# The first matmuls of a down projection set between the last two products of an FFN part

## The chip, the cores and the metric

The kernel runs on one core of a Trainium2 chip. The metric is the device time of one execution in microseconds (us), the median of several runs. Engines are called by their short names: PE is the matmul engine (PEld its weight loads), ACT the scalar engine, DVE the vector engine, POOL the GpSimd engine, SP the engine whose queue issues the DMAs here.

## What is computed

The program is one inference step of a two-layer decoder. Each layer is a mixer, an FFN and a gated addition, for 576 token columns (512 of a prompt, 64 of samples) and a model width of 1024. The change lies in the FFN:

```python
def _swiglu(x, w1, w3, w2):
    return (jax.nn.silu(x @ w1) * (x @ w3)) @ w2

x = x + _swiglu(_rmsnorm(x, W['g_ffn'][i]), W['ffn_w1'][i], W['ffn_w3'][i], W['ffn_w2'][i])
# D_MODEL = 1024, D_FF = 2816, DEPTH = 2
```

The residual `x` is held as eight tiles of 128 rows (features) by 576 columns (tokens). All of it is float32.

## The kernel before, in words

**Precision.** Every float32 operand of a matmul is split into a high part (a rounded copy made by ACT) and a low part (the rest, made by DVE), and each product is three matmuls: high by high, low by high, high by low. `split_to` (L159, L160) does so for activations, `wsplit` (L174, L175) for weights: one ACT copy of 128x1024 into `whi`, one DVE subtraction into `wlo`. There are two buffers of each of `whi` and `wlo`, two of `wraw` (the weights as they land), two accumulators of two PSUM banks (`mm`, `mmx`) and one buffer each of the sums `a0` to `a3` and `u`.

**The up half.** The 22 tiles of the hidden width are worked in 11 pairs p. For each pair seven block products are made instead of eight (a Strassen scheme over the halves of tokens and of the inner width): the products with the operands b11, b21, b2, b1, b3, b4 and b22, each 24 matmuls of 288 columns (`prod`, L1120). Those with b11, b2, b3 and b4 add into the same accumulator (`mmx`); b21 goes to `mmy`, b1 and b22 to `mmz`. The weights of b2, b1, b3 and b22 are sums of loaded blocks, made by DVE (L1157, L1158, L1163, L1173) from a11, a12, a21, a22 (buffers a0, a1, a2, a3). Before b4 may add into `mmx`, ACT has to copy out what stands there (`copied`, L1125), since the copy is a result of its own. Between b3 and b4 the program puts the first product of the next pair (`head(p + 1)`), which works in the other accumulator.

**The down half.** The pairs are grouped in three parts (`PARTS`: 4, 4 and 3 pairs). After the last pair of a part the product with w2 follows: for each of eight output tiles m, `gemm` (matmuls at L210) loads and splits the block of w2, makes 48 matmuls (36 in the third part) over the part's eight (six) hidden tiles k, and `add_out` (L361) adds the two halves of the accumulator to x on DVE. The last operand k comes from the last product, b22, through a chain on DVE and ACT (L1135, L1136, L1138, L159, L160). The last pair of a part has no next head to put between b3 and b4.

**Order.** A list scheduler with a model of the engines sets the order on every engine queue, from the program's order and its own estimate of when each instruction can start; each engine then runs its queue in that order, and SP its DMAs. The two loops run in the two layers, so there are six parts, each with its last pair and its down half.

Of the kernel before, what the change touches and what calls it, by code (L numbers as in the profile page):

```python
# [12 lines left out]
F = mybir.dt.float32  # L13
R = mybir.dt.float32r
# [5 lines left out]
P = 128  # L20
D = 1024
KD = D // P
# [4 lines left out]
HF = T // 2  # L27
# [53 lines left out]
def trunk(ctx, tc, a, stop=None):  # L81
    nc = tc.nc
    V, S, G, PE = nc.vector, nc.scalar, nc.gpsimd, nc.tensor
# [82 lines left out]
    def wraw(ap, kt):  # L166
        raw = wp.tile([P, 1024], F, tag="raw", name="wraw", bufs=RAW)[:, :kt * P]
        nc.sync.dma_start(raw, ap)
        return raw
# [13 lines left out]
    def wload(ap, kt, eng=V):  # L183
        return wsplit(wraw(ap, kt), kt, wp, 2, eng=eng)
# [73 lines left out]
    def half(s):  # L258
        return slice(s * HF, (s + 1) * HF)
# [80 lines left out]
    def run(gen):  # L340
        for _ in gen:
            pass
# [10 lines left out]
    def add_out(m, ps, r=None):  # L353
        for s in range(2):
            xh, src = x[m][:, half(s)], ps[:, s]
            if r is not None:
                t = tmp("t1", 2)[:, :HF]
                V.tensor_tensor(t, src, r[:, half(s)], op=OP.mult)
                (V if m in OUT_V else G).tensor_tensor(xh, xh, t, op=OP.add)  # L359
            else:  # L360
                V.tensor_tensor(xh, src, xh, op=OP.add)  # L361
# [697 lines left out]
    def ffn(i, ha):  # L1059
        w13, w2 = a["w13"][i], a["w2"][i]  # L1060
        with tc.tile_pool(name=f"ffn{i}", bufs=1) as hp:

            def hq():
                return [hp.tile([P, 4, T], R, tag="h" + t_, name="h" + t_, bufs=2) for t_ in "hl"]

            def keep(n):
                if n < 3 or (n < 5 and i):
                    t = [ha.tile([P, 4, HF], R, tag=("bq" if n < 3 else "xb") + t_, name="b" + t_, bufs=WPRE if n < 3 else 2)
                         for t_ in "hl"]
                    return [(range(4), *t)]  # L1070
                if n < 5:
                    return [(range(2 * j, 2 * j + 2), *(ac.tile([P, 2, HF], R, tag="xc" + t_, name="b" + t_, bufs=KD // 2)
                                                        for t_ in "hl")) for j in range(2)]
                return [(range(j, j + 1), *(ac.tile([P, HF], R, tag="xa" + t_, name="b" + t_, bufs=KD)[:, None, :]
                                            for t_ in "hl")) for j in range(4)]

            def operand(n, src, scale=None):
                out = []
                for ks, hi, lo in keep(n):
                    split_to((hi, lo), src[:, ks[0]:ks[-1] + 1], scale)  # L1080
                    out += [(hi[:, j], lo[:, j]) for j in range(len(ks))]
                return out

            r = tmp("rb", 2)
            acc = tmp("acc", 1)
            for k in range(KD):
                square_add(acc, x[k], k == 0)
            rnorm([acc], D, 0, T, [(r, 1.0)])
            (xg0, t0), (xg1, t1) = ([t_.bitcast(F) for t_ in hq()] for _ in range(2))
            for xg, k0 in ((xg0, 0), (xg1, 4)):  # L1090
                for j in range(4):
                    V.scalar_tensor_tensor(xg[:, j], x[k0 + j], pcol("g_ffn", i * KD + k0 + j), r, op0=OP.mult, op1=OP.mult)  # L1092
                if k0 == 0:
                    b11 = operand(0, xg0[:, :, :HF])
            b21 = operand(1, xg1[:, :, :HF])
            d3, d2, d1, d4 = t0[:, :, :HF], t0[:, :, HF:], t1[:, :, :HF], t1[:, :, HF:]
            V.tensor_tensor(d3, xg1[:, :, HF:], xg0[:, :, HF:], op=OP.subtract)
            V.tensor_tensor(d2, d3, xg0[:, :, :HF], op=OP.add)
            b2 = operand(2, d2, -1.0)
            V.tensor_tensor(d1, xg0[:, :, :HF], xg0[:, :, HF:], op=OP.subtract)  # L1100
            b1 = operand(3, d1)
            b3 = operand(4, d3)
            V.tensor_tensor(d4, d2, xg1[:, :, :HF], op=OP.subtract)
            b4 = operand(5, d4)
            b22 = operand(6, xg1[:, :, HF:])

            def wsum(tag, src=None):
                t = hp.tile([P, 1024], F, tag=tag, name=tag, bufs=1)
                if src is not None:
                    nc.sync.dma_start(t, src)  # L1110
                return t

            def prod(outs, wts, b, first):
                wh, wl = wts
                for n in range(2):
                    for k in range(4):
                        o = slice(n * SEQ + k * P, n * SEQ + (k + 1) * P)
                        h, l = b[k]
                        for t_, (w, v) in enumerate(((wh, h), (wh, l), (wl, h))):
                            PE.matmul(outs[n], w[:, o], v, start=(first and k == 0 and t_ == 0), stop=(k == 3 and t_ == 2),  # L1120
                                      skip_group_check=not first)

            def copied(ps, tag):
                t = v2(tmp(tag, 2))
                S.activation(t, ps[:, :, :HF], AF.Copy)  # L1125
                return t

            def head(p):
                ps = pm.tile([P, 2, 512], F, tag="mm", name="mmx")
                prod([ps[:, n, :HF] for n in range(2)], wload(w13[p, 0], KD), b11, True)  # L1130
                return ps, copied(ps, "t1")

            def block(s, outs, dst, sign):
                for n in range(2):
                    V.tensor_tensor(s[:, n], s[:, n], outs[n], op=OP.add)  # L1135
                S.activation(s[:, 0], s[:, 0], AF.Silu, scale=sign)  # L1136
                if sign > 0:
                    V.tensor_tensor(dst, s[:, 0], s[:, 1], op=OP.mult)  # L1138
                else:
                    V.scalar_tensor_tensor(dst, s[:, 1], sign, s[:, 0], op0=OP.mult, op1=OP.mult)  # L1140

            for p0, p1 in PARTS:
                hs = []
                for p in range(p0, p1):
                    if p == p0:
                        ps, s1 = head(p)
                    if (p - p0) % 2 == 0:
                        hh, hl = hq()
                    o = 2 * ((p - p0) % 2)
                    xo = [ps[:, n, :HF] for n in range(2)]  # L1150
                    ys = [bank("mmy")[:, :HF] for _ in range(2)]
                    prod(ys, wload(w13[p, 1], KD), b21, True)
                    f1, f2 = tmp("rb", 2), tmp("t2", 2)
                    block(s1, ys, f1[:, :HF], 1.0)
                    a21, a22, a11, a12 = (wsum(f"a{n}", w13[p, n]) for n in (2, 3, 0, 1))
                    u = wsum("u")
                    V.tensor_tensor(a22, a22, a21, op=OP.add)  # L1157
                    V.tensor_tensor(u, a22, a11, op=OP.add)  # L1158
                    prod(xo, wsplit(u, KD, wp, 2), b2, False)
                    s2 = copied(ps, "t2")  # L1160
                    zs = [bank("mmz", "o")[:, :HF] for _ in range(2)]
                    prod(zs, wsplit(a22, KD, wp, 2), b1, True)
                    V.tensor_tensor(a21, a21, a11, op=OP.add)  # L1163
                    prod(xo, wsplit(a21, KD, wp, 2), b3, False)
                    s3 = copied(ps, "t1")
                    block(s3, zs, f2[:, HF:], -1.0)
                    if p + 1 < p1:
                        nxt = head(p + 1)
                    prod(xo, wload(w13[p, 3], KD), b4, False)
                    S.activation(f2[:, :HF], xo[0], AF.Silu, scale=-1.0)  # L1170
                    V.scalar_tensor_tensor(f2[:, :HF], xo[1], -1.0, f2[:, :HF], op0=OP.mult, op1=OP.mult)
                    split_to((hh[:, o + 1], hl[:, o + 1]), f2)
                    V.tensor_tensor(u, u, a12, op=OP.add)  # L1173
                    prod(zs, wsplit(u, KD, wp, 2), b22, False)
                    block(s2, zs, f1[:, HF:], 1.0)
                    split_to((hh[:, o], hl[:, o]), f1)
                    hs += [(hh[:, o + 1], hl[:, o + 1]), (hh[:, o], hl[:, o])]
                    ps, s1 = nxt
                for m in range(KD):
                    add_out(m, gemm(w2[m][:, 2 * p0 * P:2 * p1 * P], hs, False))  # L1180

    def ple_up(i, pa_at, hp=None):
        pa = []
# [275 lines left out]
```

## Time and profile before

| | us |
|---|---|
| median of 3 runs | 1875.71 (1874.99 to 1875.91) |
| the profiled execution, its own time | 1873.93 |
| its span, first to last instruction | 1872.2 |
| PE busy | 1748.0 (93%) |
| DVE busy | 1343.1 (72%) |
| ACT busy | 811.7 (43%) |
| FFN of the first layer, about | 353 to 763 of the span |
| FFN of the second layer, about | 1382 to 1790 of the span |

The times in the rows below count from the start of the span. A matmul's row gives its start and its modelled end; matmuls are pipelined, so what a matmul costs is the distance to the next start, some 0.133 us here. An entry in square brackets is idle time of the engine before that row, and what ended it.

### The profile page before, as it was taken

The numbers are of one execution on the slowest core, as the hardware profiler recorded it, in microseconds if no ns is written. First come the engines' busy times: TensorE is split into PE (matmuls) and PEld (weight loads), VectorE is DVE, ScalarE is ACT, GpSimd is POOL, SyncE is SP. The second block draws the span as 40 slices with busy tenths as digits, with TensorE's granted clock in tenths as the row PEclk, the third lists the DMA queues.
The fourth block names the chain that finished last, engine by engine and source line by source line (L and its number), as shares of the span: only waits on it lengthen the run. The fifth ranks groups of instructions, "written<-read, shape, count | busy, mean of one in ns | idle before, by whom it ended". The sixth has DMA issues, their size and how long they took to land. (4 is left out here: it accounts for less than half of the span.)

```text
span 1872.2 us, 32247 instructions
## 1 busy us (share of the span) xinstructions
PE 1748.0 (93%) x13134; PEld 1693.6 (90%) x13134; DVE 1343.1 (72%) x2256; ACT 811.7 (43%) x1341; POOL 415.1 (22%) x393
## 2 busy tenths in 40 slices
PE   7899989899999999989998999998959999999994
PEld 7789979899999999989987999998959999999994
DVE  6877784886377375588996897988587637737556
ACT  6654442554254143444553444535444325415332
POOL 2433343000000000033445537455510000000002
PEclk9999999899999999989998999999979999999997
DMA  5111113244244242312231322223315424424221
GB/s 191 57 62 66 68 49 130 83 160 139 91 162 154 87 147 71 118 41 72 103 111 68 109 104 85 96 100 108 118 52 167 133 86 168 147 91 144 71 80 51
DMA packets 63124, 193.74 MB, mean 103 GB/s; under 512 B 7040, under 2 KB 12800, under 8 KB 62976
## 3 DMA queue, kind: packets, MB, share of 16 engines
q1 hardware_dynamic: 62400, 191.10, 29.8%
q8 instruction: 103, 1.69, 0.4%
q10 hardware_dynamic: 576, 0.59, 0.1%
q14 instruction: 45, 0.37, 0.1%
HBM read 177.10 MB, written 14.56 MB: 102 GB/s over the span
## 5 line engine op out<-in xcount | busy, mean ns | idle before, releaser
L174 ACT ACTIVATE whi<-wraw 128x1024 fp32r<-128x1024 f32 (+2 forms) x213 | 221.5, 1040 | 392.6 <-PE mm L210 175.3
L175 DVE TENSOR_TENSOR wlo<-wraw,whi 128x1024 fp32r<-128x1024 f32 (+1 forms) x187 | 230.4, 1232 | 73.8 <-ACT whi L174 73.0
L1220 POOL TENSOR_TENSOR ev<-ev,rb 128x288 f32<-128x288 f32 x18 | 18.1, 1034 | 952.7 <-ACT rb L255 952.7
L1120 PE MATMUL mmx<-bh,whi 128*128 128x288 f32 x704 | 211.9, 301 | 14.8 <-ACT t L1125 9.3
L1120 PE MATMUL mmx<-bh,wlo 128*128 128x288 f32 x704 | 210.6, 299 | 4.8 <-DVE wlo L175 4.7
L1120 PE MATMUL mmx<-bl,whi 128*128 128x288 f32 x704 | 210.6, 299 | 2.9 <-DVE bl L163 2.9
L193 PE MATMUL mm<-xah,whi 128*128 128x288 f32 x632 | 191.4, 303 | 3.7 <-DVE hz L264 1.7
L193 PE MATMUL mm<-xal,whi 128*128 128x288 f32 x632 | 190.2, 301 | 0.0
L193 PE MATMUL mm<-xah,wlo 128*128 128x288 f32 x632 | 189.4, 300 | 0.0
L361 DVE TENSOR_TENSOR x<-mm,x 128x288 f32<-128x288 f32 x128 | 52.4, 451 | 169.1 <-PE mm L210 159.1
L193 PE MATMUL mm<-xch,whi 128*128 128x288 f32 x536 | 161.4, 301 | 2.9 <-DVE x L361 2.9
L193 PE MATMUL mm<-xch,wlo 128*128 128x288 f32 x536 | 160.8, 300 | 0.0
L193 PE MATMUL mm<-xcl,whi 128*128 128x288 f32 x536 | 160.7, 300 | 0.0
L210 PE MATMUL mm<-hl,whi 128*128 128x288 f32 x704 | 152.0, 296 | 0.0
L210 PE MATMUL mm<-hh,whi 128*128 128x288 f32 x704 | 151.7, 296 | 0.0
L210 PE MATMUL mm<-hh,wlo 128*128 128x288 f32 x704 | 151.3, 296 | 0.0
L1120 PEld LDWEIGHTS mmx<-bh,whi 128*128 128x128 f32 x704 | 134.5, 191 | 16.9 <-ACT t L1125 10.7
L1120 PEld LDWEIGHTS mmx<-bh,wlo 128*128 128x128 f32 x704 | 135.2, 192 | 6.6 <-DVE wlo L175 6.5
L1120 PEld LDWEIGHTS mmx<-bl,whi 128*128 128x128 f32 x704 | 134.9, 192 | 3.1 <-DVE bl L163 3.1
L193 PEld LDWEIGHTS mm<-xah,whi 128*128 128x128 f32 x632 | 120.0, 190 | 7.8 <-ACT lt L497 2.1
L193 PEld LDWEIGHTS mm<-xal,whi 128*128 128x128 f32 x632 | 120.2, 190 | 2.4 <-issue 1.8
L193 PEld LDWEIGHTS mm<-xah,wlo 128*128 128x128 f32 x632 | 120.1, 190 | 1.6 <-issue 0.9
(495 smaller groups left out, 4927.4 us busy)
## 6 DMA issues: line engine op xcount, KB each, us to landing
wraw<-w SPq DMA_DIRECT2D x98, 512.0 KB, 3.4
a<-w SPq DMA_DIRECT2D x88, 512.0 KB, 3.3
wraw<-w_sin SPq DMA_DIRECT2D x40, 512.0 KB, 3.3
wraw<-w_ein SPq DMA_DIRECT2D x22, 512.0 KB, 3.3
wraw<-wg SPq DMA_DIRECT2D x16, 512.0 KB, 3.2
s<-ss SPq DMA_DIRECT2D x16, 512.0 KB, 3.5
sss<-s SPq DMA_DIRECT2D x16, 512.0 KB, 2.8
wraw<-w_sout SPq DMA_DIRECT2D x16, 512.0 KB, 3.6
```

The source lines that it names most:

```text
L174: S.activation(hi, raw, AF.Copy)
L175: eng.tensor_tensor(lo, raw, hi.bitcast(F), op=OP.subtract)
L193: PE.matmul(ps, w[:, cols], v, start=(k == 0 and i == 0), stop=(k == n - 1 and i == 2))
L210: PE.matmul(ps[:, s, :HF], w[:, j * P:(j + 1) * P], m[:, half(s)], start=(k == 0 and i == 0), stop=(k == n - 1 and i == 2))
L361: V.tensor_tensor(xh, src, xh, op=OP.add)
L1120: PE.matmul(outs[n], w[:, o], v, start=(first and k == 0 and t_ == 0), stop=(k == 3 and t_ == 2), skip_group_check=not first)
L1220: eng.tensor_tensor(v, v, r[:, half(s)], op=OP.mult)
```

## The change

A generator `down` takes the place of the loop over `gemm`. In the last pair of a part, where there is no next head, its first step runs: the weights of output tile 0 are loaded and split into two buffers of the sums, a3 and a0 (`w2a3`, `w2a0`), and its matmuls for k = 0 to 3 stand in the program between b3 and b4. After the last product come the rest of tile 0 but the last k, then tile 1 but its last k, then the last k of tile 0, its addition to x, the last k of tile 1 and its addition. Tiles 2 to 7 are as before. The number of matmuls, splits, loads and additions is the same.

```diff
+            def down(p0, p1, hs):
+                def part(m, wts, ps, ks):
+                    for k in ks:
+                        h, l = hs[k]
+                        for t_, (w, v) in enumerate(((wts[0], h), (wts[0], l), (wts[1], h))):
+                            for s_ in range(2):
+                                PE.matmul(ps[:, s_, :HF], w[:, k * P:(k + 1) * P], v[:, half(s_)],
+                                          start=(k == 0 and t_ == 0), stop=(k == n - 1 and t_ == 2))
+
+                n = 2 * (p1 - p0)
+                got = []
+                for m in range(KD):
+                    raw = wraw(w2[m][:, 2 * p0 * P:2 * p1 * P], n)
+                    if m:
+                        wts = wsplit(raw, n, wp, 2)
+                    else:
+                        wts = split_to([hp.tile([P, 1024], R, tag=t_, name="w2" + t_, bufs=1)[:, :n * P] for t_ in ("a3", "a0")], raw)
+                    ps = pm.tile([P, 2, 512], F, tag="mm", name="mm")
+                    got.append((m, wts, ps))
+                    if m == 0:
+                        part(*got[0], range(4))
+                        yield
+                        part(*got[0], range(4, n - 1))
+                    elif m == 1:
+                        part(*got[1], range(n - 1))
+                        for g in got:
+                            part(*g, [n - 1])
+                            add_out(g[0], g[2][:, :, :HF])
+                    else:
+                        part(*got[m], range(n))
+                        add_out(m, ps[:, :, :HF])
+
             for p0, p1 in PARTS:
                 hs = []
+                dn = down(p0, p1, hs)
...
                     if p + 1 < p1:
                         nxt = head(p + 1)
+                    else:
+                        next(dn)
                     prod(xo, wload(w13[p, 3], KD), b4, False)
...
-                for m in range(KD):
-                    add_out(m, gemm(w2[m][:, 2 * p0 * P:2 * p1 * P], hs, False))
+                run(dn)
```

**What the scheduler makes of it.** On PE, first part of the first layer, at the end of b3 (weights `whi_4501`), before; b4 reads `whi_4537`:

```order
L1120 MATMUL mmx_4289<-bh_3577,whi_4501 128x288
L1120 MATMUL mmx_4289<-bl_3578,whi_4501 128x288
L1120 MATMUL mmx_4289<-bh_3577,wlo_4502 128x288
L1120 MATMUL mmx_4289<-bh_3584,whi_4537 128x288
L1120 MATMUL mmx_4289<-bl_3585,whi_4537 128x288
```

And of the change, the same place (`mm_4541` is output tile 0; b4 now reads `whi_4568`):

```order
L1120 MATMUL mmx_4289<-bh_3577,wlo_4502 128x288
L1148 MATMUL mm_4541<-hh_3649,w2a3_4537 128x288 x2
L1148 MATMUL mm_4541<-hl_3650,w2a3_4537 128x288 x2
L1148 MATMUL mm_4541<-hh_3649,w2a0_4538 128x288 x2
...
L1148 MATMUL mm_4541<-hh_4143,w2a0_4538 128x288 x2
L1148 MATMUL mm_4541<-hh_4143,w2a3_4537 128x288 x2
L1120 MATMUL mmx_4289<-bh_3584,whi_4568 128x288
```

Sixteen rows of two matmuls, 32 in all, now stand between b3 and b4 (k = 0 to 4 and the first two of k = 5; in the third part of a layer 24, four of them after the second matmul of b3).

On PE, where the first two output tiles end and the third begins, before (`mm_4604`, `mm_4661`, `mm_4718` are tiles 0, 1, 2):

```order
L210 MATMUL mm_4604<-hl_4144,whi_4607 128x288 x2
L210 MATMUL mm_4604<-hh_4143,wlo_4608 128x288 x2
L210 MATMUL mm_4661<-hh_3649,whi_4664 128x288
...
L210 MATMUL mm_4661<-hl_4144,whi_4664 128x288 x2
L210 MATMUL mm_4661<-hh_4143,wlo_4665 128x288 x2
L210 MATMUL mm_4718<-hh_3649,whi_4721 128x288 x2
```

And of the change (`mm_4541`, `mm_4659`, `mm_4724` are tiles 0, 1, 2):

```order
L1148 MATMUL mm_4541<-hh_4143,w2a3_4537 128x288 x2
L1148 MATMUL mm_4659<-hh_4143,whi_4655 128x288 x2
L1148 MATMUL mm_4541<-hl_4144,w2a3_4537 128x288 x2
L1148 MATMUL mm_4541<-hh_4143,w2a0_4538 128x288 x2
L1148 MATMUL mm_4659<-hl_4144,whi_4655 128x288 x2
L1148 MATMUL mm_4659<-hh_4143,wlo_4656 128x288 x2
L1148 MATMUL mm_4724<-hh_3649,whi_4720 128x288 x2
```

Between the last matmul of tile 0 and the first of tile 2, which takes tile 0's accumulator, there stood 35 matmuls of tile 1, and now there stand four.

On DVE, at the same place, before (`hl_4144` is the low part of the last operand, x0 to x2 the first residual tiles):

```order
L160 TENSOR_TENSOR hl_4144<-rb_4423,hh_4143 128x576
L361 TENSOR_TENSOR x0_75<-mm_4604,x0_75 128x288 x2
L175 TENSOR_TENSOR wlo_4722<-wraw_4719,whi_4721 128x1024
L361 TENSOR_TENSOR x1_76<-mm_4661,x1_76 128x288 x2
L175 TENSOR_TENSOR wlo_4779<-wraw_4776,whi_4778 128x1024
L361 TENSOR_TENSOR x2_77<-mm_4718,x2_77 128x288 x2
```

And of the change:

```order
L160 TENSOR_TENSOR hl_4144<-rb_4423,hh_4143 128x576
L361 TENSOR_TENSOR x0_75<-mm_4541,x0_75 128x288 x2
L361 TENSOR_TENSOR x1_76<-mm_4659,x1_76 128x288 x2
L175 TENSOR_TENSOR wlo_4778<-wraw_4775,whi_4777 128x1024
L1190 TENSOR_TENSOR a3_5135<-a3_5135,a2_5133 128x1024
L1191 TENSOR_TENSOR u_5141<-a3_5135,a0_5137 128x1024
L1196 TENSOR_TENSOR a2_5133<-a2_5133,a0_5137 128x1024
L361 TENSOR_TENSOR x2_77<-mm_4724,x2_77 128x288 x2
L175 TENSOR_TENSOR wlo_4835<-wraw_4832,whi_4834 128x1024
```

The three sums of the next part's first pair (L1190, L1191, L1196; before they stood as L1157, L1163 and L1158 around b4) have moved behind the addition of tile 1, because they need the buffers a3 and a0, which hold tile 0's weights until its last matmul. In SP's queue the loads into a3 and a0 have moved likewise, and the load of tile 0's weights stands one place earlier than before, ahead of that of b4's.

## Rows read from the trace of the kernel before

**Rows 1.** The page, busy time, share of the span and instructions.

```profile
PE 1748.0 (93%) x13134; PEld 1693.6 (90%) x13134; DVE 1343.1 (72%) x2256; ACT 811.7 (43%) x1341; POOL 415.1 (22%) x393
```

**Rows 2.** Stretch around a part's end: us, busy, granted PE clock, DMA.

```profile
440.00:466.00 26.00, 24.45 (x184) 24.21 (x183) 17.27 (x25) 10.75 (x16) 0.00 (x0) 1.00 0.44 143
```

**Rows 3.** Waits of PE by what ended them: us in total, times, longest.

```profile
PE mmx L1120 <- ACT t L1125: 9.3, 6, 1.6
...
PE mm L193 <- DVE x L361: 2.9, 3, 2.2
```

**Rows 4.** Timeline, PE: last of b3, b4, end of b22, tile 0.

```profile
448.32 0.29 PE L1120 MATMUL mmx<-bh,wlo 128*128 128x288 f32 x1
450.17 0.40 PE L1120 MATMUL mmx<-bh,whi 128*128 128x288 f32 x1 [1.55 <-ACT t L1125]
450.41 0.30 PE L1120 MATMUL mmx<-bl,whi 128*128 128x288 f32 x1
...
456.50 0.29 PE L1120 MATMUL mmz<-bh,wlo 128*128 128x288 f32 x1
456.64 0.42 PE L210 MATMUL mm<-hh,whi 128*128 128x288 f32 x2
```

**Rows 5.** Timeline, ACT, around b3 and b4 of that pair.

```profile
443.16 0.64 ACT L1125 ACTIVATE t<-mmx 128x576 f32<-128x576 f32 x1
445.32 1.06 ACT L174 ACTIVATE whi<-wraw 128x1024 fp32r<-128x1024 f32 x1 [1.52 <-PE mmz L1120]
448.52 1.06 ACT L174 ACTIVATE whi<-u 128x1024 fp32r<-128x1024 f32 x1 [2.14 <-PE mmx L1120]
449.48 0.63 ACT L1125 ACTIVATE t<-mmx 128x576 f32<-128x576 f32 x1
```

**Rows 6.** Timeline, DVE, the same pair and the first addition.

```profile
443.29 1.23 DVE L175 TENSOR_TENSOR wlo<-a,whi 128x1024 fp32r<-128x1024 f32 x1 [0.70 <-ACT whi L174]
446.41 1.23 DVE L175 TENSOR_TENSOR wlo<-wraw,whi 128x1024 fp32r<-128x1024 f32 x1 [1.89 <-ACT whi L174]
448.20 1.22 DVE L1157 TENSOR_TENSOR a<-a,a 128x1024 f32<-128x1024 f32 x1 [0.56 <-DMA a<-w]
...
460.28 0.76 DVE L160 TENSOR_TENSOR hl<-rb,hh 128x576 fp32r<-128x576 f32 x1 [0.75 <-ACT hh L159]
464.94 0.82 DVE L361 TENSOR_TENSOR x<-mm,x 128x288 f32<-128x288 f32 x2 [3.91 <-PE mm L210]
465.82 1.23 DVE L175 TENSOR_TENSOR wlo<-wraw,whi 128x1024 fp32r<-128x1024 f32 x1
```

**Rows 7.** Timeline, PE: the last two matmuls of tile 0.

```profile
464.48 0.43 PE L210 MATMUL mm<-hh,wlo 128*128 128x288 f32 x2
```

**Rows 8.** Timeline, PE, in the mixer: an accumulator awaited from additions.

```profile
315.20 0.29 PE L193 MATMUL mm<-xch,wlo 128*128 128x288 f32 x1
315.88 0.40 PE L193 MATMUL mm<-xch,whi 128*128 128x288 f32 x1 [0.38 <-DVE x L361]
316.11 0.29 PE L193 MATMUL mm<-xcl,whi 128*128 128x288 f32 x1
```

**Rows 9.** Timeline, PEld, at the wait of rows 4.

```profile
450.17 0.19 PEld L1120 LDWEIGHTS mmx<-bh,whi 128*128 128x128 f32 x1 [1.79 <-ACT t L1125]
```

**Rows 10.** Timeline, SP: loads of b4's weights, an a block, tile 0's weights.

```profile
429.46 0.33 SPq L168 DMA_DIRECT2D wraw<-w  x1
432.82 0.33 SPq L1110 DMA_DIRECT2D a<-w  x1
434.93 0.33 SPq L168 DMA_DIRECT2D wraw<-w  x1
```

**Rows 11.** DMA issues, KB, median us to landing: the page; 441.5 to 441.8; 316 to 318.2.

```profile
wraw<-w SPq DMA_DIRECT2D x98, 512.0 KB, 3.4
...
a<-w SPq DMA_DIRECT2D x1, 512.0 KB, 5.3
...
a<-w SPq DMA_DIRECT2D x4, 512.0 KB, 7.6
```

**Rows 12.** Timeline, DVE and PE, second layer: a sum waiting for its load.

```profile
1454.33 1.22 DVE L1157 TENSOR_TENSOR a<-a,a 128x1024 f32<-128x1024 f32 x1 [2.37 <-DMA a<-w]
...
1458.01 0.40 PE L1120 MATMUL mmx<-bh,wlo 128*128 128x288 f32 x1 [1.61 <-DVE wlo L175]
```

## The prediction

> **What bounds the kernel now.** I read the shares of busy time first: PE works 93% of the span, twenty points above DVE [rows 1]. A microsecond counts if PE stands still in it. So next come PE's waits by what ended them. One line there belongs to this change alone: six waits of 1.6 us at most and 9.3 us in sum on ACT's copy of an accumulator, L1125 [rows 3], and there are six last pairs of a part. The timeline shows one of them. The last matmul of b3 starts at 448.32, b4's first at 450.17 and its second at 450.41 [rows 4]. Two steps of 0.133 us would be 0.27 us; they took 2.09, so the place costs **1.82 us**, of which 1.55 is called idle and the rest is the slow restart. The reason stands on ACT: b3 ends, ACT first makes the high part of the next weights (448.52, it had waited for b3 to free that buffer), then at 449.48 the copy [rows 5]. Later, where the down half begins, PE does not stand still: b22's last matmul starts at 456.50 and tile 0's first at 456.64 [rows 4]. The last operand is ready at 461.04 (460.28 + 0.76 [rows 6]), before the matmuls reach it. So the gain is in the hole between b3 and b4, and the operand at the end of b22 gives none.
>
> **What it removes.** In the first part 32 matmuls of tile 0 fill the hole, 32 x 0.133 = 4.27 us of work that is needed anyway; in the third part of a layer 24, 3.2 us. ACT's copy was done 1.79 us after b3's last start (449.48 + 0.63 against 448.32), so both cover it and b4 then finds its accumulator free. Gain: 6 x 1.82 = **10.9 us**, if tile 0's weights are there at 448.45. They are: their load takes the place in SP's queue of b4's, issued at 429.46 [rows 10], and weights land in 3.4 us [rows 11]. The move puts b4's own load into the place at 434.93, still 10 us ahead of its split. The ACT copy that makes the high part, 1.06 us, falls between the copy that ends at 443.80 and the split at 445.32, where ACT was idle for 1.52 us; DVE's subtraction, 1.23 us, falls into its idle 1.89 us before 446.41 [rows 5, 6]. Both are hidden, by 0.46 and 0.66 us. If that cover were gone, PE would wait for them in the new place and b4's weights, split behind them, would have some two further microseconds until 452.7.
>
> **What it moves without cost.** The end of b22 shifts to 448.45 + (32 + 24 + 24) x 0.133 = 459.1. Tile 1's weights need the buffer of b4, free at 456.1; copy and subtraction take 1.06 + 1.23, so 458.5, and PE asks at 459.6. The chain from b22 to the last operand took 4.4 us (456.64 to 461.04), so it ends at 463.6 or, with a DVE subtraction in its way, 464.7; the first matmul of k = 7 comes 52 matmuls behind b22, at 466.0. In the third part 36 matmuls stand there, 4.8 us against at most the same 4.4. No wait, but there the margin is below 1 us.
>
> **What it adds.** Tile 2 takes the accumulator of tile 0. Before, 35 matmuls of tile 1 stood between the two; now there are four. So PE waits for both additions of tile 0. In the trace the first begins 0.33 us after tile 0's last matmul started (464.48 plus one step is 464.61, the addition 464.94), and the pair takes 0.82 us [rows 6, 7]: it ends 1.15 us after that start. PE reaches tile 2 after five steps, 0.67 us. That leaves 0.48 us, and a restart. The row nearest to it is in the mixer, where PE waits for an accumulator from the same additions: 315.20 to 316.11 is 0.91 us for two steps, 0.64 too much [rows 8]. I take **0.64 us**, 6 x 0.64 = 3.8 us. The lower bound is none, if PE were released by other means; the upper one is 0.64 plus one DVE instruction of a weight's size, 1.14 us, if one stands in front.
>
> The restart is 0.10 us of each such wait (450.17 to 450.41 instead of 0.133), and the weight load belonging to it begins at 450.17 too, after idling for 1.79 us [rows 9]. The Trainium skill (TensorE: Matmul & The Clock Gate, the table at its head) says that PE's queue pulls weight loads ahead of matmuls in flight. By that rule the load would be done when the wait ends, and the cost would be 6 x 0.1 = 0.6 us less, 1868.0 instead of 1868.6. The row disagrees with that reading: the load waits along with its matmul.
>
> The second thing added is on DVE and SP. The next part's loads into a3 and a0 now wait for tile 0's last matmul, the sums of them stand on DVE behind the addition of tile 1, and behind the sums stand the addition of tile 2 and the low part of tile 4's weights. Taking first part times: tile 0's last matmul starts at 448.45 + 139 x 0.133 = 467.0. The loads go out from 467.4 on; one among others took 5.3 us [rows 11], which gives 473.6 for the second if it is issued at 468.3. The three sums, 1.14 us each, then end at 476.9 at the latest. Tile 2 starts at 468.2 and ends at 474.8; its addition slips to 477.7, the split for tile 4 to 478.9. PE asks for tile 4 at 468.2 + 96 x 0.133 = 481.0. Nobody waits, with **2.1 us** in hand. This holds in four parts; the third part of a layer has no next pair. At the next part's start nothing is late: its second operand's sum was asked for 45 us later.
>
> **The sum.** 10.9 - 3.8 = 7.1 us less. What PE gains is kept, since behind a part it works without a hole to the next head, and granted clock is 1.00 around the part's end [rows 2]. Against the profiled execution, 1873.93 us (span 1872.2 and 1.7 around it), that is 1866.8. That execution was 1.8 us below the median of the runs, 1875.71; against the median I predict **1868.6 us**.
>
> **Rivals.**
>
> *A longer wait for tile 0's accumulator, the gain is given back (1875.4).* If DVE has one instruction of a weight's size in front of the additions, each part pays 0.64 + 1.14 = 1.78 us, 10.7 in all, and 0.2 us remains. For it: in the trace before a split follows the first addition at once [rows 6], and a wait of 2.2 us on such additions exists [rows 3]. Against it: in the new order the additions stand right behind the last operand's low part. A wait for both tiles' additions, 1.4 us a part, gives 1873.1 and belongs here too.
>
> *No wait for the accumulator (1864.8).* PE is 10.9 us faster, if the operand's lateness or a later tile 1 spaces the matmuls so that the additions are through. Against it: four matmuls last half as long as the additions.
>
> *The next part's sums hold DVE (slower).* DVE stands at L1190 or L1191 until a load lands, and the split for tile 4 stands behind. The trace shows exactly that at another place: DVE waits 2.37 us for a load and PE 1.61 us for the split behind it [rows 12]. Here it decides once the second load lands later than 473.6 + 2.1 = 475.7, 7.4 us after an issue at 468.3; each us more costs four parts 4 us. To use up the 7.1 us and pass 0.2% (3.75 us) takes 10.85 / 4 = 2.7 us beyond that, 10.1 us to land. With 10.6 us: 4 x 3.2 = 12.8 us, or 1881.4. Against it: the slowest group in the rows, four such loads issued within 2.2 us, took 7.6 us in the median [rows 11], and here two are out together. The Trainium skill (PSUM — Partial Sum Buffer, Engine vs sequencer instructions) calls the vector engine's queue strictly first in, first out; by that rule nothing passes the waiting sum, and rows 12 agree.
>
> *It does not do what it says (1879.5).* Tile 0's weights are late and PE waits before them instead of before b4; the hole stays and 3.8 us of new wait comes on top. Against it: the idle time on ACT and DVE and a load 10 us early.
>
> **How the numbers follow.** Forecast 0.68, no wait 0.06, longer wait 0.16, sums that hold DVE 0.06, weights late 0.04. About 0.2% (3.75 us) is what a measurement of this kernel can tell from no change, so faster has the first two, 0.74; within 0.2% the third, 0.16; slower the last two, 0.10. The range runs from the case without a wait, 1864.8, to 1873.4, past the wait for both additions (1873.1); what lies above is the rest of the longer wait and the two slower cases.
>
> **What would show it.** Right: in the profile after, PE's line of waits on L1125 is without its six entries of 1.55 us; six new waits of 0.3 to 0.5 us idle on the addition to x appear where tile 2 begins; PE goes through b3, tile 0, b4 and b22 without idle time; and DVE waits for an a load behind tile 1's addition with no PE wait behind it. Wrong: idle PE before the first matmul of tile 0 or before b4, at k = 7 of tiles 0 and 1 (above all in the third parts), a wait on the accumulator near 1.8 us, or one on the weights of tile 4.

## The result, and the profile after

The changed kernel takes **1865.63 us** (median of 4 runs, 1864.96 to 1867.17), the kernel before 1875.35 us on the same chip (4 runs, 1874.83 to 1875.91): a ratio of 0.9949, 95% interval 0.9932 to 0.9967, or 9.7 us less. The profiled execution of after took 1867.17 us. In a later set of runs the same pair gave 0.9960 (0.9946 to 0.9975), 7.5 us less; why the two differ is taken up below.

The head of the page of after, as in [rows 1], says little by itself: PE does the same work in a span that is 6.8 us shorter.

```profile
span 1865.4 us, 32243 instructions
PE 1746.9 (94%) x13134; PEld 1691.6 (91%) x13134; DVE 1343.2 (72%) x2256; ACT 810.9 (43%) x1341; POOL 416.3 (22%) x393
```

PE's waits by what ended them (sum in us, times, longest), to be held against [rows 3]: the line of six waits on ACT's copy, L1125, is gone, and a line stands there that before did not have, six waits of PE on the additions to x.

```profile
PE mmx L1120 <- DVE wlo L175: 4.2, 6, 1.3
...
PE mm L1148 <- DVE x L361: 2.3, 6, 0.4
```

The timeline of PE shows both places of the first part (start, length, and in brackets the idle time before the row). The first rows answer to [rows 4]: b3's last matmul at 449.04, tile 0's first at 449.17, one step of 0.13 us on, and no bracket. The last rows are the start of tile 2: 468.82 is 0.68 us after the second matmul of the row at 468.01 (468.14).

```profile
449.04 0.29 PE L1120 MATMUL mmx<-bh,wlo 128*128 128x288 f32 x1
449.17 0.42 PE L1148 MATMUL mm<-hh,w2a 128*128 128x288 f32 x2
449.43 0.42 PE L1148 MATMUL mm<-hl,w2a 128*128 128x288 f32 x2
...
467.47 0.43 PE L1148 MATMUL mm<-hh,w2a 128*128 128x288 f32 x2
467.74 0.43 PE L1148 MATMUL mm<-hl,whi 128*128 128x288 f32 x2
468.01 0.43 PE L1148 MATMUL mm<-hh,wlo 128*128 128x288 f32 x2
468.82 0.54 PE L1148 MATMUL mm<-hh,whi 128*128 128x288 f32 x2 [0.39 <-DVE x L361]
469.19 0.42 PE L1148 MATMUL mm<-hl,whi 128*128 128x288 f32 x2
```

ACT still makes the weight copy first and the accumulator's copy second, as in [rows 5]; that costs nothing now, since tile 0 keeps PE busy meanwhile.

```profile
449.24 1.06 ACT L174 ACTIVATE whi<-u 128x1024 fp32r<-128x1024 f32 x1 [2.14 <-PE mmx L1120]
450.20 0.63 ACT L1125 ACTIVATE t<-mmx 128x576 f32<-128x576 f32 x1
```

DVE around the start of tile 2: the last operand's low part (463.42), four additions in one row (tile 0 and tile 1), the low part of tile 3's weights, the next part's three sums with one short wait for a load, and then 0.82 us in which DVE waits for PE.

```profile
463.42 0.76 DVE L160 TENSOR_TENSOR hl<-rb,hh 128x576 fp32r<-128x576 f32 x1 [0.75 <-ACT hh L159]
467.94 1.55 DVE L361 TENSOR_TENSOR x<-mm,x 128x288 f32<-128x288 f32 x4 [3.76 <-PE mm L1148]
469.41 1.22 DVE L175 TENSOR_TENSOR wlo<-wraw,whi 128x1024 fp32r<-128x1024 f32 x1
471.03 1.23 DVE L1190 TENSOR_TENSOR a<-a,a 128x1024 f32<-128x1024 f32 x1 [0.41 <-DMA a<-w]
472.33 1.23 DVE L1191 TENSOR_TENSOR u<-a,a 128x1024 f32<-128x1024 f32 x1
473.47 1.22 DVE L1196 TENSOR_TENSOR a<-a,a 128x1024 f32<-128x1024 f32 x1
475.51 0.82 DVE L361 TENSOR_TENSOR x<-mm,x 128x288 f32<-128x288 f32 x2 [0.82 <-PE mm L1148]
```

**A yardstick that scatters less than the run.** To weigh edits of a microsecond I cut the same work out of every trace: the last 144 matmuls of a part's up half and all of its matmuls with w2, 528 in sum (432 in the third part), from the start of the first to the start of the last. In the rows below (stretch, its length, busy time and count of each engine, granted clock, DMA) the first is the kernel before, the second the changed one, the third the version with banks of its own that comes below. They hold the same work, at a granted clock of 1.00, which is the higher of its two levels (2.4 GHz).

```profile
435.68:507.67 71.99, 70.44 (x530) 70.20 (x528) 34.72 (x48) 19.70 (x25) 0.00 (x0) 1.00 0.34 110
```
```profile
436.39:507.18 70.79, 70.41 (x529) 70.17 (x528) 34.74 (x48) 19.61 (x25) 0.00 (x0) 1.00 0.36 120
```
```profile
435.17:505.30 70.13, 70.13 (x530) 70.13 (x529) 34.82 (x48) 19.60 (x25) 0.00 (x0) 1.00 0.36 121
```

The lengths of the six stretches in us, by the starts in the timeline, for every kernel that was run (the sums are of the unrounded lengths):

| kernel | first layer, parts 1 to 3 | second layer, parts 1 to 3 | sum | against before |
|---|---|---|---|---|
| before | 71.99, 71.99, 59.20 | 72.02, 72.02, 59.24 | 406.46 | |
| the change | 70.79, 70.79, 58.00 | 70.73, 70.73, 57.94 | 398.97 | -7.5 |
| the change again | 70.80, 70.79, 57.98 | 70.72, 70.73, 57.93 | 398.95 | -7.5 |
| filling alone | 70.78, 70.78, 57.98 | 70.74, 70.72, 57.93 | 398.92 | -7.5 |
| late operand alone | 72.34, 72.34, 59.92 | 73.26, 73.28, 59.94 | 411.08 | +4.6 |
| own banks | 70.13, 70.12, 57.34 | 70.08, 70.08, 57.27 | 395.01 | -11.4 |
| own weight buffer | 70.76, 70.76, 59.24 | 70.95, 70.75, 59.23 | 401.69 | -4.8 |
| ACT's copy first | 71.19, 71.19, 58.40 | 71.19, 71.38, 58.41 | 401.77 | -4.7 |
| change in the first layer | 70.78, 70.79, 57.99 | 72.01, 72.02, 59.24 | 402.82 | -3.6 |
| own banks, second layer | 70.78, 70.78, 57.98 | 70.07, 70.09, 57.27 | 396.97 | -9.5 |
| own banks, five parts | 70.13, 70.13, 57.97 | 70.08, 70.08, 57.27 | 395.65 | -10.8 |
| own banks, first layer | 70.12, 70.13, 57.34 | 70.72, 70.72, 57.92 | 396.94 | -9.5 |

### The profile page after: what moved, and what is told of

It reads as the page before. It is cut to its first block, busy times and chain, and to the rows that moved or that the text cites. A ratio compares the mean times of both kernels' runs of the same rounds, so it can differ in the third digit from the quotient of the medians.

```text
span 1865.4 us, 32243 instructions
## 1 busy us (share of the span) xinstructions
PE 1746.9 (94%) x13134; PEld 1691.6 (91%) x13134; DVE 1343.2 (72%) x2256; ACT 810.9 (43%) x1341; POOL 416.3 (22%) x393
## 5 line engine op out<-in xcount | busy, mean ns | idle before, releaser
L174 ACT ACTIVATE whi<-wraw 128x1024 fp32r<-128x1024 f32 (+2 forms) x207 | 215.5, 1041 | 389.5 <-PE mm L1148 156.7
L175 DVE TENSOR_TENSOR wlo<-wraw,whi 128x1024 fp32r<-128x1024 f32 (+1 forms) x181 | 223.7, 1236 | 83.7 <-ACT whi L174 83.0
L1148 PE MATMUL mm<-hh,whi 128*128 128x288 f32 x616 | 133.9, 297 | 2.3 <-DVE x L361 2.3
L1148 PE MATMUL mm<-hl,whi 128*128 128x288 f32 x616 | 132.4, 296 | 0.0
L1148 PE MATMUL mm<-hh,wlo 128*128 128x288 f32 x616 | 132.3, 296 | 0.0
```

Source lines behind the costliest of these rows:

```text
L174: S.activation(hi, raw, AF.Copy)
L175: eng.tensor_tensor(lo, raw, hi.bitcast(F), op=OP.subtract)
L1148: PE.matmul(ps[:, s_, :HF], w[:, k * P:(k + 1) * P], v[:, half(s_)], start=(k == 0 and t_ == 0), stop=(k == n - 1 and t_ == 2))
```

## The experiments

The theory on record: filling the hole gains 1.82 us in each of six parts, and handing tile 0's accumulator to tile 2 too early costs 0.64 us in each. The rivals say that the gain or the loss sits elsewhere. Ratios are to runs of the kernel before on the same chip, with 95% intervals; a gain in us is read from the ratio unless the medians are named.

**The change again.** No edit; the same kernel in the same set of runs as the next three.

> The changed kernel as it is, once more beside the kernel before, to size what is to be explained. The sum of the prediction (six holes of 1.82 us less six new waits of 0.64 us) gives 7.1 us less than before, ratio 0.9962. The first runs gave 9.7 us less, 0.9949. If the first is the whole story, five rounds come out near 0.996; if some 2.6 us come from elsewhere, near 0.995.

Measured: 1868.23 us against 1874.45 (before: 12 runs, 1870.6 to 1876.89), ratio 0.9960 (0.9946 to 0.9975), 7.5 us less. Its six stretches are those of the first profile within 0.02 us each, 7.5 us below before in sum. So 7.5 us is what the change does to these places, and the 2.2 us by which the first comparison showed more are not in them. The runs of one kernel scatter by some 6 us, from 1870.6 to 1876.89 for before, and the first comparison's interval reaches down to a gain of 6.2 us. By the run times alone both ratios of the expectation, 0.996 and 0.995, stay possible; it is the stretches that decide. Outside the FFNs PE's rows stand in the same order in the traces before and after.

**Filling alone.** The first four k of tile 0 stand in the hole, but the last operand is not put off; the program goes through the tiles in order.

```diff
                     got.append((m, wts, ps))
+                    part(*got[m], range(4))
                     if m == 0:
-                        part(*got[0], range(4))
                         yield
-                        part(*got[0], range(4, n - 1))
-                    elif m == 1:
-                        part(*got[1], range(n - 1))
-                        for g in got:
-                            part(*g, [n - 1])
-                            add_out(g[0], g[2][:, :, :HF])
-                    else:
-                        part(*got[m], range(n))
-                        add_out(m, ps[:, :, :HF])
+                    part(*got[m], range(4, n))
+                    add_out(m, ps[:, :, :HF])
```

> Only the first half of the change: tile 0's first four k stand between b3 and b4, and every tile then takes its last operand in its own place in the program. Theory (the gain is the filled hole): the scheduler still puts 32 matmuls in the hole, and, as the last operand is late, it sets tile 1's matmuls before tile 0's end by itself, with four of tile 1 behind tile 0's last; so the same six waits of 0.4 us on the addition, and the time of the changed kernel within 1 us. Rival (taking the last operand late brings a part of its own, up to the 2.6 us that the sum does not explain): slower than the changed kernel by up to 2.6 us, with PE waits on the last operand at k = 7.

Measured: 1867.77 us, ratio 0.9964 (0.9949 to 0.9978), stretches within 0.02 us of the change's. PE's waits are the change's too:

```profile
PE mm L1148 <- DVE x L361: 2.3, 6, 0.4
```

The scheduler by itself puts off tile 0's last matmuls behind matmuls of tile 1, so that the program's second edit hardly moves a row of PE's queue: filling the hole is the whole change, and the wait for the accumulator comes with it, whether the deferral is written down or not.

**Late operand alone.** The deferral without the filling: tile 0 starts behind b22, with weights in the ordinary buffers.

```diff
-                    if m:
-                        wts = wsplit(raw, n, wp, 2)
-                    else:
-                        wts = split_to([hp.tile([P, 1024], R, tag=t_, name="w2" + t_, bufs=1)[:, :n * P] for t_ in ("a3", "a0")], raw)
+                    wts = wsplit(raw, n, wp, 2)
...
-                        yield
...
-                    else:
-                        next(dn)
...
-                run(dn)
+                down(p0, p1, hs)
```

> Only the second half of the change: nothing stands between b3 and b4, tile 0's weights take an ordinary buffer, and tiles 0 and 1 take the last operand at their end. Theory: the six holes of 1.82 us stay; tile 2 now finds both the accumulator and the weight buffer of tile 0 free only after its end. Its high part is ready about 1.4 us after tile 0's last matmul starts, its low part, behind the four additions, about 3.2 us after, while PE asks for it after 2.0 us; with restarts some 1.6 us a part, so 6 x 1.6 = 9.6 us slower than before, about 1885. Rival (the late operand pays by itself): faster than before, by up to 2.6 us.

Measured: 1881.54 us, ratio 1.0038 (1.0024 to 1.0051), 7.1 us more than before. By itself the edit is a loss, though less of one than the 9.6 us expected. PE's waits show the old hole, untouched, and three new lines at tiles 2 and 3: both weight buffers and both accumulators come free together, at the end of tile 1.

```profile
PE mmx L1120 <- ACT t L1125: 9.3, 6, 1.6
PE mm L1148 <- ACT whi L174: 0.8, 4, 0.2
PE mm L1148 <- DVE wlo L175: 0.7, 4, 0.2
PE mm L1148 <- DVE x L361: 0.4, 2, 0.2
```

These are small, and each brings a restart. In the stretch of the first part the three waits step 0.50, 0.40 and 0.45 us and the matmul behind each 0.21, 0.24 and 0.24, where 0.133 is usual: 2.04 - 6 x 0.133 = 1.24 us. The first two parts of the second layer are longer by 1.24 and 1.26 us, as that says, those of the first layer by 0.35 us only (there the other matmuls followed each other a little faster, at 131.4 ns in the mean for 133.1, which over some 520 of them makes up the other 0.9 us); why, stays open. The third parts show two such waits and 0.7 us. So the places cost 0.35 to 1.26 us a part, not the 1.6 expected. The stretches hold 4.6 of the 7.1 us; the rest was not located, and lies within the scatter of the runs (the interval begins at 4.5 us).

**Own banks.** The change, but tile 0 adds up in two single PSUM banks, those in which the product with b21 stood earlier in the pair and which are idle by then. So tile 2 takes an accumulator that is long free, and no further bank is used.

```diff
-                    ps = pm.tile([P, 2, 512], F, tag="mm", name="mm")
+                    ps = pm.tile([P, 2, 512], F, tag="mm", name="mm") if m else [bank("mm0") for _ in range(2)]
+                    ps = [ps[:, s_, :HF] for s_ in range(2)] if m else [b_[:, :HF] for b_ in ps]
...
-                                PE.matmul(ps[:, s_, :HF], w[:, k * P:(k + 1) * P], v[:, half(s_)],
+                                PE.matmul(ps[s_], w[:, k * P:(k + 1) * P], v[:, half(s_)],
```

> The whole change, but tile 0 adds up in the two single banks that the products with b21 use (idle from the middle of a pair on), not in one of the two accumulators; so tile 2 need not wait for the addition of tile 0. Theory: the six waits on the addition (2.3 us idle, 3.8 us with restarts) go, and nothing else changes: 3.8 us faster than the changed kernel, 10.9 us or, with the unexplained rest, up to 13.5 us faster than before, 1861.9 to 1864.5. Rival (the wait hides another one that is due at the same place, the weights of tile 2 or the last operand): within 1 us of the changed kernel, with a wait of another name in the same six places.

Measured: **1854.65 us** (1854.38 to 1855.39), ratio 0.9897 (0.9884 to 0.9909), by the medians 19.8 us less than before, more than expected. The six waits at L1148 are gone, and the stretches answer exactly: 11.45 us below before, 3.96 us below the change, 0.66 us a part. In the first part's stretch PE is busy in all of its 70.13 us (third row above). So the hole was worth 1.86 us a part in the first layer and 1.94 to 1.97 in the second, and the wait 0.66. The further 8 us had to lie elsewhere. The part of the span between the two FFNs, from the last matmul with w2 of the first to the first product of the second, is 617.9 us long here, and 624.1 in the change: the scheduler had set the second layer's mixer in another order on all five queues. The last two experiments separate that from the banks.

**Own weight buffer.** The change, with tile 0's weights in a new buffer and a1 instead of a3 and a0, so that the next part's loads into a3 and a0 and the sums of them need not wait for tile 0.

```diff
-... for t_ in ("a3", "a0")], raw)
+... for t_ in ("h", "a1")], raw)
```

> The change as it is, but tile 0's weights stand in a buffer of their own and in a1, so that the next part's loads into a3 and a0 and their sums no longer wait for tile 0's last matmul. Theory: those sums had cover, nobody waits for them; the time is that of the changed kernel within 1.5 us, some 7.5 us below before (ratio 0.996), and PE's six waits of about 0.38 us idle on the addition to x stay. Rival: the sums behind tile 1's addition cost the changed kernel something; then this one is a further 2 us or more below it (ratio 0.995 or less).

Measured: 1870.26 us, ratio 0.9975 (0.9964 to 0.9985). In the four parts with a next part the stretches are 70.76, 70.76, 70.95 and 70.75 for the change's 70.79, 70.79, 70.73 and 70.73: the sums behind tile 1's addition cost the change nothing, and the rival falls. But the third parts lost their gain, 59.24 and 59.23 for 58.00 and 57.94, which the theory had not foreseen. The scheduler put sixteen of tile 0's matmuls ahead of b3's end, eight before b3 and eight into it, and four were left for the hole (which of its choices did that was not followed). In the timeline of the first layer's third part b3 ends, four matmuls of tile 0 run, and PE again waits for ACT's copy, which ends at 713.45:

```profile
711.66 0.29 PE L1120 MATMUL mmx<-bh,wlo 128*128 128x288 f32 x1
711.79 0.42 PE L1148 MATMUL mm<-hl,w2h 128*128 128x288 f32 x2
712.05 0.42 PE L1148 MATMUL mm<-hh,w2a 128*128 128x288 f32 x2
713.51 0.40 PE L1120 MATMUL mmx<-bh,whi 128*128 128x288 f32 x1 [1.03 <-ACT t L1125]
```
```profile
712.82 0.63 ACT L1125 ACTIVATE t<-mmx 128x576 f32<-128x576 f32 x1
```

It confirms the count by accident: what fills a hole has to be left for it.

**ACT's copy first.** Nothing of w2 is moved. In the last pair of a part ACT copies the accumulator ahead of the high part of b22's weights.

```diff
-                S.activation(t, ps[:, :, :HF], AF.Copy)
+                copies.append(S.activation(t, ps[:, :, :HF], AF.Copy).ins)
...
-                    prod(zs, wsplit(u, KD, wp, 2), b22, False)
+                    with tc.issue_after(copies[-1]) if p + 1 == p1 else ExitStack():
+                        wu = wsplit(u, KD, wp, 2)
+                    prod(zs, wu, b22, False)
```

> The kernel before with one edit: in the last pair of a part ACT's copy of b3's accumulator, L1125, stands ahead of the high part of b22's weights. Nothing of w2 is moved. Theory (the hole of 1.82 us is ACT's order: 0.96 us of weight copy stand ahead of the copy that PE waits for): the six waits remain but shrink by about 0.96 us each, to 0.6 us idle, and the time falls by 6 x 0.96 = 5.8 us (ratio 0.9969), since b22's weights have b4's 6.4 us as cover. Rival (the copy would have begun no earlier, since b3's end and not ACT's order sets it): the waits stay at 1.55 us and the time is that of before, ratio 1.000.

Measured: 1871.35 us, ratio 0.9981 (0.9970 to 0.9991), 3.6 us less; the stretches give 4.7 us, and PE's six waits on L1125 shrink from 9.3 us [rows 3] to 4.4:

```profile
PE mmx L1120 <- ACT t L1125: 4.4, 6, 0.7
```

The 5.8 us expected were not reached. In the timelines ACT now begins the copy at 447.66 and PE b4 at 448.37:

```profile
447.66 0.65 ACT L1125 ACTIVATE t<-mmx 128x576 f32<-128x576 f32 x1 [2.27 <-PE mmx L1120]
448.21 1.05 ACT L174 ACTIVATE whi<-u 128x1024 fp32r<-128x1024 f32 x1
```
```profile
448.37 0.40 PE L1120 MATMUL mmx<-bh,whi 128*128 128x288 f32 x1 [0.74 <-ACT t L1125]
```

b3's last matmul starts at 447.34, 1.03 us before b4, so the copy begins 0.32 us after it, where it began 1.16 us after it in [rows 4, 5]. That is 0.84 us earlier, not 0.96: the weight copy had begun 0.20 us after that start, the accumulator's copy begins only 0.32 us after it. The reading of the ACT rows holds: about half of the hole was the order of two instructions on ACT, and it is to be had without moving a matmul.

**Change in the first layer alone.** The branch with `next(dn)` and the call of `run(dn)` are taken in layer 0; layer 1 keeps the old loop.

```diff
-                    else:
+                    elif i == 0:
                         next(dn)
```

> The change in the first layer's feed-forward block alone. Theory (six equal places, three in each layer): half the gain, 3.5 to 4 us below before, ratio 0.998; three waits of 1.5 us on L1125 remain in the second layer and three waits of 0.38 us on the addition to x stand in the first. Rival (part of the gain is a shift of loads and work outside the block): the gain is all or nothing, 0.996 or 1.000.

Measured: 1869.86 us against 1875.10, ratio 0.9969 (0.9957 to 0.9982). The median is 5.2 us lower, and the interval, 3.4 to 8.1 us, takes in the 3.5 to 4 expected, but the rival's 0.996 too. The stretches decide: they give 3.6 us less, all of it in the first layer, and those of the second are as before within 0.01 us. So the gain is not all or nothing. PE's waits are three of each kind:

```profile
PE mmx L1120 <- ACT t L1125: 4.7, 3, 1.6
PE mm L1148 <- DVE x L361: 1.2, 3, 0.4
```

**Own banks in the second layer alone.** As own banks, with `if m or i == 0`. Up to the second FFN all five queues have the change's order.

> The change, with two PSUM banks of its own for tile 0's accumulator in the second layer's feed-forward block alone; up to that block all engines have the changed kernel's order. Theory: three waits of 0.38 us idle (0.64 to 0.68 us with the restart) on the addition to x go, 2.0 us below the changed kernel, and with the 7.1 of the change some 9 to 9.5 us below before (ratio 0.995); what the version with own banks in both layers gained beyond 11 us came from the order of the second mixer between the blocks, which moved with it, so it does not show here. Rival: the own banks themselves gain more than the waits, about half of the 19.8 us: 13 us or more below before (ratio 0.993 or less).

Measured: 1866.21 us, ratio 0.9955 (0.9942 to 0.9969), 8.4 us less; stretches 9.5 us less, 2.0 below the change, 0.64 to 0.67 a part. As the theory said; a gain of 13 us lies outside the interval.

**Own banks in five parts.** All but the third part of the first layer. ACT and POOL keep the change's order throughout, PE, DVE and SP but for the instructions that write and read tile 0's accumulator and a few others that stand some places away (five matmuls on PE, one product on DVE, one load on SP).

> The change, with banks of its own for tile 0's accumulator in five of the six parts: all but the third of the first layer. The second mixer between the blocks then has the changed kernel's order on PE, DVE, ACT and POOL. Theory (each wait for the accumulator costs 0.64 us, and the rest of the 19.8 us was the order of the mixer): 7.1 + 5 x 0.64 = 10.3 us below before, ratio 0.9945; one wait of 0.38 us on the addition to x stays, in the third part of the first layer. Rival (the own banks gain more in the blocks than the waits): 7.1 + 5/6 x 12.7 = 17.7 us below before, ratio 0.9906.

Measured: 1863.51 us against 1877.46, ratio 0.9935 (0.9917 to 0.9954). That is 12.2 us less, 8.6 to 15.6 by the interval: 10.3 lies in it, 17.7 does not. The stretches give 10.8, and one wait on the addition to x is left, of 0.4 us.

**Own banks in the first layer.** Three parts only, but with the mixer's new order.

> The change, with banks of its own for tile 0's accumulator in the first layer alone. Only three waits go, but the second mixer takes the order that it has with own banks in both layers. Theory (the mixer's order is worth some 5.5 us by itself): 7.1 + 3 x 0.64 + 5.5 = 14.5 us below before, ratio 0.9923, and PE is not waiting on the recurrence of the second mixer at the three or four places between 830 and 985 us where the changed kernel loses 1.6 to 2.2 us. Rival (the order of the mixer is worth nothing): 9 us, ratio 0.9952.

Measured: 1859.37 us against 1877.46, ratio 0.9915 (0.9895 to 0.9936): 16.0 us less, with the 14.5 of the theory inside the interval (12.0 to 19.7) and the 9 of the rival outside. The stretches hold 9.5 of it. Most of the rest is in the mixer. One stretch of it, from the first matmul with a low part `xcl` (L1318 in the one, L1319 in the other) to a broadcast at L252, with the same 1241 matmuls and 291 DVE instructions, in the changed kernel and in this one:

```profile
830.70:1003.72 173.02, 158.26 (x1241) 149.52 (x1241) 149.22 (x291) 79.10 (x159) 64.44 (x80) 0.95 0.25 86
```
```profile
829.36:995.06 165.70, 155.54 (x1241) 147.32 (x1241) 151.12 (x291) 78.91 (x159) 61.56 (x80) 0.96 0.28 89
```

It is 7.3 us shorter. With own banks in both layers it is 166.17 us; in the ten traces with the old order, own banks in five parts among them, it takes 171.1 to 173.1. Of the 7.3 us, 4.6 are time in which PE stood still (14.8 us there, 10.2 here), and 2.7 are that the same matmuls were busy for less, at a granted clock of 0.96 in the mean for 0.95. Some of PE's waits in it, first of the changed kernel, then of this one: the wait of 2.2 us for `ys` at L941 is gone and one of 0.5 for `st` stands at that line, that for `gm` is 1.0 us shorter, that for `up` is gone, and one for `E` is 1.0 us longer; smaller ones make up the rest.

```profile
PE us L941 <- DVE ys L936: 2.2, 1, 2.2
PE bts L861 <- DVE gm L849: 1.6, 1, 1.6
PE mm L193 <- DVE up L125: 0.9, 1, 0.9
...
PE yp L977 <- DVE E L966: 0.4, 1, 0.4
```
```profile
PE yp L977 <- DVE E L966: 1.4, 1, 1.4
PE bts L861 <- DVE gm L849: 0.6, 1, 0.6
PE us L941 <- DVE st L926: 0.5, 1, 0.5
```

So of the 19.8 us of own banks, 11.4 are the six places of this case, and some 6 go with another order of another stage that the scheduler fell into (617.9 and 617.3 us between the FFNs with that order, 620.9 to 624.7 in the ten traces without it). The 2 us that remain were not located. Which of the scheduler's choices tipped was not followed.

## Why the prediction was right

- **The hole, 1.82 us.** Right: 1.86 us in the first layer, 1.94 to 1.97 in the second, 11.4 in sum for the 10.9 of the prediction (in the second layer most of the excess is in the usual steps, whose mean went from 133.2 to 133.0 ns). Filled as said: tile 0's first matmul follows b3's last by one step, so its weights were there, and the two splits of them on ACT and DVE stayed hidden. Neither tile 0 nor b4 nor b22 has a step above 0.15 us.
- **The wait for the accumulator, 0.64 us.** Right in place, cause and size. Tile 0's last matmul starts at 467.60, the additions at 467.94 (0.33 us predicted), and tile 2 starts at 468.82; step and restart are 0.68 + 0.24 - 2 x 0.133 = 0.65 us, and taking the wait away gave 0.66 a part, 3.96 us in sum for 3.8. The rival of a longer wait falls: on DVE nothing stands before the four additions, and PE was released after the second of them, whose pair ends at 468.76. The rival without a wait falls too.
- **The net gain.** 7.1 us predicted, 7.5 in the stretches of two executions. The size of the first comparison, 9.7 us, is not explained by this working and was not repeated; it is scatter between runs as far as these runs tell. Some sums of the prediction are off by 0.1 us (463.6 for 463.5, 1873.1 for 1873.2, 1875.4 for 1875.5), which changes none of its conclusions.
- **The last operand.** b3's last matmul starts 0.72 us later here than in the trace that the prediction worked from (449.04 for 448.32), so times are counted from it. Predicted ready after 15.3 to 16.4 us, measured after 15.1 (464.18, that is 463.42 + 0.76); predicted to be wanted after 17.7, and tile 0 takes it after 17.6 (466.67). In the third part it is ready at 724.16 and tile 0 wants it at 725.14, 1.0 us of margin. The prediction reckoned with 4.8 - 4.4 = 0.4 there; the chain took 3.8 us (720.37 to 724.16).
- **The next part's sums.** Counted in the same way, predicted loads from 19.1 us on and sums done by 28.6 at the latest; the loads went out after 18.6 us (467.66) and the last sum ended after 25.7 (473.47 + 1.22). DVE then waited 0.82 us for PE before tile 2's addition, and 0.74, 0.78 and 0.80 us in the other three parts that have a next one, so no addition slipped at all. The rival needed a second load of over 7 us; it landed after 4.2 us here, and the waits for loads were 0.49 us at most. At the next part's start ACT split the sum that is asked for first, `u`, at 510.58, some 36 us after the last of the three had ended; the 45 us of the prediction stand on no row shown, but the cover is there. The own weight buffer shows the same from the other side.
- **The weight load behind the wait.** PEld's row at the start of tile 2 is the one below: it begins at the same moment as its matmul, after 0.62 us of idle time. As in [rows 9], the load did not run ahead of the matmul that waited, and the restart of 0.10 us was paid: 0.24 us to the second matmul (469.06).

```profile
468.82 0.30 PEld L1148 LDWEIGHTS mm<-hh,whi 128*128 128x128 f32 x2 [0.62 <-DVE x L361]
```

What the prediction did not see is how much more was to be had: the wait that it priced could have been kept out by letting tile 0 add up in the two banks that the product with b21 leaves idle.

## What to carry to other kernels

A hole of PE between two dependent products is filled by any work that has its operands, and its worth is read from two starts in the timeline (here 2.09 us for two steps of 0.133); but ask at once which buffer the filling work holds longer than before, and who takes it next, since that wait gave back a third of the gain. Before moving work, look whether the engine that releases the wait does something else first: one instruction's place on ACT was worth 4.7 of the 11.4 us. Where a scheduler orders the program, a small edit can shift another stage by as much as itself, so compare stretches of equal work in two traces and not the run times alone.

## What the runs showed that was not expected

- Executions of one kernel scatter by 6 to 11 us (before: 1870.6 to 1876.89 in one set, 1870.3 to 1881.32 in another), while the stretches above repeat within 0.02 us in every kernel that has the same order there. PE's waits for the low part of weights in the products, which often stand behind a load, took between 1.5 us (own banks in five parts) and 5.1 us (own banks in the first layer) of a span, not always at the same places. That is a part of the scatter; not all of it was located.
- Each wait of PE that was looked at, however short, brings a second, slow step: 0.21 to 0.24 us to the next matmul where 0.133 is usual. Three waits of 0.10 to 0.21 us idle cost 1.24 us in the experiment on the late operand.
